# Layer 0's gates by seven quarter products per pair of blocks beside the retention, and its keys, queries and values beside the state space

## The chip, the cores and the metric

The kernel runs on one core of one Trainium2 chip. TensorE multiplies, VectorE (DVE in the profile), ScalarE (ACT) and GpSimd (POOL) do elementwise work, SyncE (SP) issues every DMA of the kernel, in program order, and 16 DMA engines move the bytes. The metric is the device time of one execution in microseconds; 1208.52 is the median of 3 runs of the kernel before (1208.01 to 1209.64).

## The reference

Input x is 1024 frames by 1024 features in float32. Layer 0 normalises x, projects it once (`proj = h @ w_in`) and cuts the result into six parts: the state-space input and its gate (1024 columns each), queries and keys (512 each), values and the retention gate (1024 each).

```
u_s5, g_s5, q, k, v, g_ret = jnp.split(h @ w_in, cuts, axis=-1)
y_s5  = s5_mixer(u_s5, ...) * silu(g_s5)          # state space, gelu, then y * sigmoid(y @ glu_w + glu_b)
y_ret = retention(rope(q), rope(k), v) * silu(g_ret)   # 8 heads, normalised per head
x = x + concat([y_s5, y_ret]) @ w_out
```

Layer 1 is a convolution module with its own projections. A last normalisation gives the output. All of it is float32, and every large product must keep about float32 accuracy.

## The kernel before, in words

Everything lies transposed: 128 features on the partitions, time along the row, so that a block of 128 output features by 512 frames fills one PSUM bank. The 1024 frames make two halves h. Each operand is split into a high part that TensorE's fast float32 format holds exactly and a low part that is the rest; `mm3` (L161) multiplies a 128x128 block of weights with 512 frames in three matmuls: high by high (L166), high weight by low operand (L167), low weight by high operand (L168). `gemm` runs `mm3` over the 8 blocks of the inner dimension, 24 matmuls for one bank. Weights come by `wnext` and `wload` (L105, L114), a list `wseq` in the order of use, two loads ahead: one DMA of 512 KB (tile wf), the high part by ScalarE (wh), the low part by GpSimd or, for the names in `LO_V`, by VectorE (wl). wf, wh and wl have three buffers each.

The work of layer 0 goes in these stages:

- **Front** (`layer0_front`): x is loaded, scaled by norm_g and split into the operands `xs[h][kb]`, 32 tiles of 256 KB that live in the pool opA under the tags A0 (first half) and A1 (second half). The factor of the normalisation (R, along the frames) is multiplied in after the products. Eight blocks of state-space input (u) are made.
- **State space** (`s5_states`, `s5_out`, eight blocks B of 128 features), and beside it the 16 blocks of both gates (`gate_block` in `layer0_front`, two to each B): 48 matmuls of 512 frames to a block, the evacuation by VectorE times R (L349), Silu by ScalarE (L350), a store of 512 KB (L353) to `gs_d` or `gr_d` in DRAM. The blocks' outputs go to `y_d`, and `k_d` holds small tables (Kt) that are stored and read back spread out (Wd).
- **Retention** (`retention`), four pairs of heads. For each pair `ret_proj` makes keys and queries (a `gemm` per half, then the rotation, for which rows are swapped by DMA inside SBUF); values of pairs 0 and 1 come from `ret_values_wide` (matmuls of 512 columns, L930 to L932), those of pairs 2 and 3 from `ret_values` (256 columns, L910 to L912). `y_pass` (L806) reads the state space's output, applies gelu and stores `yn_d`. `ret_heads` (L938) does the attention of two heads (tiles ktp, kv, sp, ro, rt), normalises, multiplies by the gate read from `gr_d` (L998, L1041), and stores `yr_d`.
- **GLU and output projection** (`layer0_back_and_layer1`): `load_split` reads yn_d (operands of the GLU) and later yr_d back, splits them into opA; 16 GLU products follow in the order of blocks nb with both halves h each, with the gate read from `gs_d` (yg, L1094) and multiplied by GpSimd (L1097); then the output projection reads both.

Layer 1 follows. The order of each engine's instructions is decided when the program is built, by a scheduler that goes by priorities and estimated times; each engine then runs its own list strictly in order and waits at semaphores.

## Time and profile before

| | before |
|---|---|
| median of the runs | 1208.52 us |
| span of the profiled execution | 1211.5 us |
| beside the state space (110 to 336 us): TensorE busy | 226.0 of 226 us |
| retention (336 to 590 us): TensorE busy | 252.6 of 254 us |
| GLU and after (590 to 655 us): TensorE busy | 65.0 of 65 us |
| DMA share and rate, 110 to 336 | 0.35, 122 GB/s |
| DMA share and rate, 336 to 590 | 0.59, 187 GB/s |
| DMA share and rate, 655 to 760 | 0.76, 262 GB/s |
| bytes moved by DMA | 227.12 MB |

The span is from the first to the last instruction of one profiled execution; it is its own time, and the median above is of other runs of the same program without a profile. A stage's row counts busy time inside a stretch of the span. The DMA share is the mean busy share of the 16 DMA engines, and the rate is what they moved. Matmuls are pipelined, so that TensorE's busy time overlaps from one to the next; a gap in it is idle time, but a full stretch does not say how fast matmuls follow each other.

### The profile page before, as it was taken

How to read it: one execution, taken by the hardware profiler on the slowest of the kernel's cores; microseconds unless marked ns; L12 is line 12 of the kernel's file. 1: busy time of each engine (PE TensorE's matmuls, PEld its weight loads, DVE VectorE, ACT ScalarE, POOL GpSimd, SP SyncE). 2: the span in 40 equal slices, each digit the busy share in tenths (PEclk: the TensorE clock that was granted, in tenths of full speed). 3: DMA queues.
4: the chain of work that ended last, by engine and by line, in shares of the span. 5: the costliest groups of instructions: out<-in, count | busy, mean ns of one | idle time of the engine just before them, and what ended most of it. 6: DMA issues, size and time to landing. Idle time of an engine off the chain costs nothing.

```text
span 1211.5 us, 17261 instructions
## 1 busy us (share of the span) xinstructions
PE 1199.2 (99%) x6478; PEld 1005.8 (83%) x6478; DVE 756.7 (62%) x1353; ACT 479.7 (40%) x706; POOL 626.5 (52%) x441
## 2 busy tenths in 40 slices
PE   9999999999999999999999999999999999999997
PEld 7888888888888889998888888888888888888877
DVE  7965655555412456457546422699999799899533
ACT  7212233332223232144334322545535675434652
POOL 2059988888236253242341110678453567758642
PEclk9999999999999999999999999999999999999998
DMA  9342433333385175467447886765678654356773
GB/s 334 105 140 72 138 131 136 127 125 141 107 279 181 53 216 141 166 208 257 144 151 235 308 273 218 243 204 201 217 248 276 204 194 153 112 192 234 243 261 131
DMA packets 100516, 227.12 MB, mean 187 GB/s; under 512 B 9296, under 2 KB 38224, under 8 KB 99792
## 3 DMA queue, kind: packets, MB, share of 16 engines
q1 hardware_dynamic: 100432, 226.01, 55.7%
q8 instruction: 51, 0.84, 0.3%
q14 instruction: 33, 0.27, 0.1%
HBM read 160.51 MB, written 61.28 MB: 183 GB/s over the span
## 4 chain that ended last, share of the span: by engine, by line
PE 90%; DMA 5%; DVE 2%; ACT 1%; POOL 1%; issue 1%; SPq 0%; DVEq 0%; POOLq 0%; ACTq 0%
PE mm_g L167 7%; PE mm_g L168 7%; PE mm_g L166 7%; PE mm_wo L166 4%; PE mm_wo L168 4%; PE mm_wo L167 4%; PE mm_b L167 2%; PE mm_b L168 2%; PE mm_a L167 2%; PE mm_a L168 2%; PE mm_b L166 2%; PE mm_a L166 2%; PE mm_u L168 2%; PE mm_u L167 2%; PE mm_u L166 2%; PE mm_oc L167 2%
## 5 line engine op out<-in xcount | busy, mean ns | idle before, releaser
L1225 DVE SCALAR_TENSOR_TENSOR cv<-u,convw,cv 128x512 f32<-128x512 f32 x398 | 273.3, 750 | 12.0 <-ACT cv L1211 9.7
L1205 POOL TENSOR_TENSOR tp<-tp,tp 128x512 f32<-128x512 f32 x64 | 83.2, 1300 | 44.1 <-ACT tp L1204 43.0
L168 PE MATMUL mm_g<-xh,wl_g 128*128 128x512 f32 x256 | 100.8, 394 | 0.0
L167 PE MATMUL mm_g<-xl,wh_g 128*128 128x512 f32 x256 | 100.6, 393 | 0.0
L166 PE MATMUL mm_g<-xh,wh_g 128*128 128x512 f32 x256 | 100.5, 393 | 0.0
L1204 ACT ACTIVATE tp<-u,convw 128x512 f32<-128x512 f32 x64 | 45.7, 720 | 36.5 <-POOL tp L1205 34.9
L349 DVE TENSOR_TENSOR gt<-mm_g,R 128x512 f32<-128x512 f32 x32 | 21.9, 685 | 59.9 <-PE mm_g L168 59.9
L392 POOL TENSOR_TENSOR s1q<-s1q,s1q 128x512 f32<-128x512 f32 x12 | 17.3, 1443 | 78.0 <-ACT s1q L387 78.0
L167 PEld LDWEIGHTS mm_g<-xl,wh_g 128*128 128x128 f32 x256 | 48.1, 188 | 11.3 <-issue 1.6
L168 PEld LDWEIGHTS mm_g<-xh,wl_g 128*128 128x128 f32 x256 | 48.0, 188 | 10.6
L166 PEld LDWEIGHTS mm_g<-xh,wh_g 128*128 128x128 f32 x256 | 48.1, 188 | 9.6
L168 PE MATMUL mm_oc<-zh,wl_woc 128*128 128x512 f32 (+1 forms) x152 | 54.2, 359 | 0.9 <-DMA wl_woc<-lo_woc 0.9
L167 PE MATMUL mm_oc<-zl,wh_woc 128*128 128x512 f32 (+1 forms) x152 | 54.4, 360 | 0.5 <-POOL zl L1050 0.5
L166 PE MATMUL mm_oc<-zh,wh_woc 128*128 128x512 f32 (+1 forms) x152 | 54.1, 361 | 0.0
L1097 POOL TENSOR_TENSOR yg<-yg,yn 128x512 f32<-128x512 f32 x16 | 21.4, 1343 | 59.6 <-DMA yg<-gs_d 25.3
L167 PE MATMUL mm_u<-xl,wh_u 128*128 128x512 f32 x128 | 50.1, 391 | 0.7 <-DVE xl L281 0.6
L166 PE MATMUL mm_g<-h1h,wh_cg 128*128 128x512 f32 x128 | 50.4, 394 | 0.0
L166 PE MATMUL mm_glu<-yh,wh_glu 128*128 128x512 f32 x128 | 50.3, 393 | 0.0
L166 PE MATMUL mm_b<-h1h,wh_cb 128*128 128x512 f32 x128 | 50.2, 392 | 0.0
L166 PE MATMUL mm_wo<-yrh,wh_wor 128*128 128x512 f32 x128 | 50.2, 392 | 0.0
L168 PE MATMUL mm_a<-h1h,wl_ca 128*128 128x512 f32 x128 | 50.2, 392 | 0.0
L166 PE MATMUL mm_wo<-ysh,wh_wos 128*128 128x512 f32 x128 | 50.0, 391 | 0.1
(402 smaller groups left out, 3576.8 us busy)
## 6 DMA issues: line engine op xcount, KB each, us to landing
wf_g<-w_ab SPq DMA_DIRECT2D x16, 512.0 KB, 4.1
wf_wos<-w_out SPq DMA_DIRECT2D x16, 512.0 KB, 4.4
wf_wor<-w_out SPq DMA_DIRECT2D x16, 512.0 KB, 5.6
wf_cb<-w_c SPq DMA_DIRECT2D x16, 512.0 KB, 4.8
wf_ca<-w_c SPq DMA_DIRECT2D x16, 512.0 KB, 4.8
wf_woc<-w_out_c SPq DMA_DIRECT2D x16, 512.0 KB, 5.1
wf_v<-w_v SPq DMA_DIRECT2D x12, 512.0 KB, 5.7
wf_cg<-w_c SPq DMA_DIRECT2D x11, 512.0 KB, 4.3
```

Source lines behind the costliest of these rows:

```text
L166: nc.tensor.matmul(ps, wh[:, kb, :], xh, start=start, stop=False)
L167: nc.tensor.matmul(ps, wh[:, kb, :], xl, start=False, stop=False)
L168: self.last_mm = nc.tensor.matmul(ps, wl[:, kb, :], xh, start=False, stop=stop)
L349: nc.vector.tensor_tensor(gt[:, c], ps[:], self.R[:, c], op=ALU.mult)
L392: nc.gpsimd.tensor_tensor(a, a, sq[:], op=ALU.add)
L1097: gp.tensor_tensor(yg[:], yg[:], yn[:], op=ALU.mult)
L1204: nc.scalar.mul(sk[:], u[:, k:k + HALF], cw[:, nb, k:k + 1])
L1205: gp.tensor_tensor(s0[:], s0[:], sk[:], op=ALU.add)
L1225: v.scalar_tensor_tensor(dst[:], *tap, accs_[i][:], op0=ALU.mult, op1=ALU.add)
```

## The change

The gates are computed by seven products of quarters. Take two neighbouring blocks of gate features (weights split into the halves of the inner dimension) and the two halves of the frames: a two by two by two block product, which eight products of quarters give directly. The change uses seven (Strassen's scheme in Winograd's form), with sums of weights and sums of operands:

- `operand_sums` reads x again beside the state space, scales it by norm_g and R, and forms seven operand sets a0, b0, b1, t1 to t4 (four tiles each, of 128 by 512); each tile is split in a high and a low part (`keep`) and stored in DRAM (`x_d`). `load_set` reads a set back into the tiles of opA.
- `wload_sums` loads the two weights of a pair and forms the sums of their halves by VectorE. It does so twice, since the pairs are gone through in two sweeps: `gates_first` (weights Sa, Sb; sets a0, t2, b0, t1) and `gates_second` (Sc, Sd; sets t3, b1, t4). Partial results of the first sweep go to `part_d` in DRAM and come back in the second, except those of pair 7.
- The sweeps run beside the retention: two pairs ahead of it, the others between its pairs of heads.
- Keys, queries and values (`keys_queries`, `values`) take the gates' place beside the state space, in eight units, one to a block B; all values by matmuls of 512 columns. They are stored in `kq_d`, `v_d` and read back (`ret_rotate`, `ret_values`). The low parts of the values' weights are made by VectorE.
- Gates are stored without Silu. Silu is done by ScalarE when they are read: for the state space at the GLU, for the retention in `load_split` of yr, where GpSimd multiplies.
- The GLU starts with blocks 0 and 1 of the first half; yr's loads are issued behind the sixth and the twelfth load of gates; yn's operands are read into five smaller buffers.

```diff
+    def wload_sums(self, src, name):
...
+            if kind == "a":
+                f = self.w_first = raw(0)
+            elif kind == "b":
+                f, cols = raw(1), (B, A)
+                v.tensor_tensor(f[:, A], f[:, A], f[:, B], op=ALU.add)
+                v.tensor_tensor(f[:, B], f[:, A], self.w_first[:, A], op=ALU.subtract)
+            elif kind == "c":
+                f, g = raw(0), raw(1)
+                v.tensor_tensor(f[:, A], f[:, A], g[:, A], op=ALU.subtract)
+                v.tensor_tensor(f[:, B], f[:, B], g[:, B], op=ALU.subtract)
+                v.tensor_tensor(f[:, B], f[:, B], f[:, A], op=ALU.add)
+                self.w_second = g
+            else:
+                f, cols = self.w_second, (B,)
...
+        for c in cols:
+            h = wh[:].rearrange(fl)[:, c]
+            nc.scalar.copy(h, f[:, c])
+            nc.gpsimd.tensor_tensor(wl[:].rearrange(fl)[:, c], f[:, c], h.bitcast(F32), op=ALU.subtract)
...
-        for nb in range(8, 24):
-            B = (nb - 8) // 2
-            if nb % 2 == 0:
-                self.s5_states(B)
-            gate_block(nb, self.wnext(f"g{nb}"), self.gs_d if nb < 16 else self.gr_d)
-            if nb % 2 == 0 and B:
+        sums = self.operand_sums(xp)
+        for B in range(8):
+            self.s5_states(B)
+            nm, s = UNITS[B]
+            unit = keys_queries(s) if nm == "kq" else values(s)
+            next(unit)
+            for _ in range((B > 0) + (B > 3)):
+                next(sums, None)
+            if B:
                 self.s5_out(B - 1)
-            if nb % 2 and B < 7:
+            for _ in unit:
+                pass
+            for _ in range(2 * (B > 0)):
+                next(sums, None)
+            if B < 7:
                 self.s5_tables(B + 1)
+            if B == 5:
+                self.X = {}
+                self.load_set("a0", "A0")
+                self.load_set("t2", "A0")
         self.s5_out(7)
+        self.load_set("b0", "A1")
+        self.load_set("t1", "A1")
...
+        def keep(f, name, i):
+            hi = xp.tile([P, HALF], F32R, name=f"{name}h_{i}", tag="hi", bufs=2)
+            lo = xp.tile([P, HALF], F32R, name=f"{name}l_{i}", tag="lo", bufs=1)
+            nc.scalar.copy(hi[:], f[:])
+            v.tensor_tensor(lo[:], f[:], hi[:].bitcast(F32), op=ALU.subtract)
+            for q, t in enumerate((hi, lo)):
+                nc.sync.dma_start(self.x_d[name][i, :, q, :], t[:].bitcast(F32))
...
+    def gates_first(self, gp, i):
...
+        wa = self.wnext(f"Sa{i}")
+        x = self.bank(f"mm_g{i}x", aux=False)
+        self.product(x, wa, 0, X["a0"], True)
+        s1 = gp.tile([P, HALF], F32, name=f"gp1_{i}", tag="p1", bufs=1)
+        nc.scalar.copy(s1[:], x[:])
+        wb = self.wnext(f"Sb{i}", ahead=1)
+        z = self.bank(f"mm_g{i}z", aux=False)
+        self.product(z, wb, 1, X["t2"], True)
...
+        part(0)
+        self.wahead(2)
+        self.product(x, wa, 1, X["b0"], False)
+        t = gp.tile([P, HALF], F32, name=f"gc11_{i}", tag="gc", bufs=3)
+        nc.scalar.copy(t[:], x[:])
+        nc.sync.dma_start(self.gate_rows(i, 0)[:, :HALF], t[:])
+        self.product(z, wb, 0, X["t1"], False)
+        part(1)
...
+    def gates_second(self, gp, i):
...
+        self.product(z, wc, 0, X["t3"], True)
+        out(z, 1, 1, 1)
+        x = self.bank(f"mm_g{i}w", aux=False)
+        self.product(x, wc, 1, X["b1"], True)
+        out(x, 1, 0, 1)
+        wd = self.wnext(f"Sd{i}")
+        self.product(z, wd, 1, X["t4"], False)
+        out(z, 0, 1, 0)
...
+        chunks = [first[2:3], first[3:6],
+                  first[6:] + [lambda: self.load_parts(gp, SWEEP2[1]), lambda: sets(("t3", "A0"), ("b1", "A1"), ("t4", "A1"))], second[:4], second[4:]]
         for pair in range(4):
...
+            K, Q, qadds = self.ret_rotate(pair)
+            V = self.ret_values(pair)
+            for f in chunks[pair]:
+                f()
...
-                    v.tensor_tensor(gts[hh][:, c], tp[:], gts[hh][:, c], op=ALU.mult)
+                    nc.scalar.copy(gts[hh][:, c], tp[:])
...
+                        nc.scalar.activation(g, g, AF.Silu)
+                        gp.tensor_tensor(f, f, g, op=ALU.mult)
...
+            nc.scalar.activation(yg[:], yg[:], AF.Silu)
             gp.tensor_tensor(yg[:], yg[:], yn[:], op=ALU.mult)
```

`part(q)` adds the first product to the bank on VectorE and stores the sum (`part_d`); `out` adds the part that came back and stores the quarter of the gate. `product` is four blocks of the inner dimension, 12 matmuls.

More of the change, by code (lines that the diff above doesn't have):

```diff
@@ new lines, in load_set, with gate_rows @@
+    def load_set(self, name, tag):
+        self.X[name] = []
+        for i in range(KB // 2):
+            pair = []
+            for q in range(2):
+                t = self.op_tile(self.opA, tag, f"X{name}{'hl'[q]}_{i}")
+                self.nc.sync.dma_start(t[:].bitcast(F32), self.x_d[name][i, :, q, :])
+                pair.append(t)
+            self.X[name].append(pair)
+    def gate_rows(self, i, n):
+        dst = self.gs_d if i < 4 else self.gr_d
+        k = (2 * i + n) % 8
+        return dst[k * P:(k + 1) * P]
```

295 lines of the change are left out of this document (185 added, 110 removed).

## Prediction

> **What bounds the kernel now.** I read the page first: engine totals, the slices, the chain of work that ended last.
>
> ```profile
> span 1211.5 us, 17261 instructions
> ...
> PE 1199.2 (99%) x6478; PEld 1005.8 (83%) x6478; DVE 756.7 (62%) x1353; ACT 479.7 (40%) x706; POOL 626.5 (52%) x441
> ...
> PE   9999999999999999999999999999999999999997
> ...
> PEclk9999999999999999999999999999999999999998
> DMA  9342433333385175467447886765678654356773
> GB/s 334 105 140 72 138 131 136 127 125 141 107 279 181 53 216 141 166 208 257 144 151 235 308 273 218 243 204 201 217 248 276 204 194 153 112 192 234 243 261 131
> ...
> PE 90%; DMA 5%; DVE 2%; ACT 1%; POOL 1%; issue 1%; SPq 0%; DVEq 0%; POOLq 0%; ACTq 0%
> ```
>
> TensorE is busy 99% of the span and nine tenths or more in 39 of 40 slices, its granted clock is at nine tenths or more in the same slices, and 90% of the chain is TensorE's own work. A microsecond of matmul removed is a microsecond of time, as long as nothing else becomes late. The profiled execution has a span of 1211.5 us, 3.0 over the median of 1208.52; I sum against the span and take 3.0 off.
>
> What else could become late is read from the same columns cut by stage: the state space with the gates beside it (110 to 340), the retention with keys, queries, values (340 to 560), the GLU and the start of the output projection (560 to 700).
>
> ```profile
> core 0: us, PE busy (x) PEld busy (x) DVE busy (x) ACT busy (x) POOL busy (x), PEclk, DMA share, GB/s
> 110.00:340.00 230.00, 230.00 (x1542) 192.51 (x1543) 121.33 (x172) 70.93 (x127) 171.32 (x128) 1.00 0.36 124
> 340.00:560.00 220.00, 220.00 (x1439) 192.21 (x1437) 101.11 (x254) 68.28 (x84) 90.33 (x51) 1.00 0.58 178
> 560.00:700.00 140.00, 138.53 (x667) 115.02 (x664) 76.35 (x133) 51.86 (x76) 40.48 (x24) 0.99 0.65 226
> ```
>
> In the first two stages TensorE never waits, in the third for 1.5 us. VectorE is half busy beside the state space, ScalarE under a third, and the 16 DMA engines are busy 0.36, 0.58 and 0.65 of the time. The change spends exactly these reserves.
>
> How long does a matmul take? The "busy" of one overlaps its neighbour's, so I take start to start: by tile, then by timeline.
>
> ```profile
> L910 PE MATMUL mm_v<-wh_v,xh x128: 277/283/387, 470.1 to 552.3; 128*128 128x256 f32 x128
> ...
> L930 PE MATMUL mm_v<-wh_v,xh x64: 389/389/389, 359.2 to 402.1; 128*128 128x512 f32 x64
> ```
>
> ```profile
> 489.43 0.28 PE L911 MATMUL mm_v<-wl_v,xh 128*128 128x256 f32 x1
> ...
> 490.39 0.28 PE L910 MATMUL mm_v<-wh_v,xh 128*128 128x256 f32 x1
> ```
>
> The 512-wide products of L930 start 64 times between 359.2 and 402.1 us, with the two others of a triple between each pair: 42.9 / (63 x 3) = **0.227 us**. The 256-wide ones make 8 starts in 0.96 us: **0.120 us**, which is more than half of 0.227.
>
> **The change part by part.**
>
> *Matmuls.* Gates: 16 blocks of 48 products (768) become 8 pairs of 7 products of quarters, 12 matmuls each (672): 96 x 0.227 = 21.8 us off. Values: 384 of 256 columns (46.1 us) become 192 of 512 (43.6): 2.5 us off. Keys and queries keep their 384, and everything from the output projection on stays in the same order. The stage beside the state space keeps its length (384 + 384 matmuls in place of 768). If nothing waits: **-24.3 us**, a span of 1187.2. The products that add onto an open bank are matmuls of the same shape; I price them alike.
>
> *Operand sums beside the state space.* Each of 28 quarters is made by VectorE, rounded by ScalarE, its low part subtracted by VectorE, and both parts stored (56 DMAs of 256 KB), after 16 loads of 256 KB. What that costs VectorE:
>
> ```profile
> L349 DVE TENSOR_TENSOR gt<-mm_g,R x32: 676/682/693, 112.5 to 333.7; 128x512 f32<-128x512 f32 x32
> ```
>
> ```profile
> L158 DVE TENSOR_TENSOR wl_g<-wf_g,wh_g 128x1024 fp32r<-128x1024 f32 x13 | 20.5, 1576 | 0.9 <-ACT wh_g L157 0.9
> ...
> L735 DVE TENSOR_TENSOR m<-v,Ts 128x512 f32<-128x512 f32 x8 | 5.5, 692 | 46.3 <-PE v L727 46.3
> ```
>
> Gone are 32 evacuations (21.9 us, L349) and 13 weight subtractions (20.5 us); new are 60 operations of 512 columns (at 0.69 us, 41), 16 evacuations of keys and queries (11) and 16 weight subtractions of the values (16 x 1.58 = 25): 121 - 42 + 77 = 156 of 230 us. As a total this is hidden. As an order it may not be: the low part has **one** buffer. Each of the 28 subtractions waits until the store of the one before has landed, VectorE works in order, and behind the wait stand the evacuations of keys and queries, whose banks TensorE needs for the next values. In the changed program's order nearly all 28 stand between the last u blocks and the third unit of the eight, with 76 us of other VectorE work. Walking that stretch with these durations, each gap between two low parts lasts the longer of the work in it and the landing: 110 us with a landing of 2.2, 120 with 3.0, 137 with 4.0, against some 108 until TensorE wants the bank. How long do stores take?
>
> ```profile
> gs_d<-gt SPq DMA_DIRECT2D x8, 512.0 KB, 4.5
> ...
> gr_d<-gt SPq DMA_DIRECT2D x8, 512.0 KB, 3.4
> ...
> gs_d<-sgg SPq DMA_DIRECT2D x16, 256.0 KB, 3.6
> ...
> outT<-fo SPq DMA_DIRECT2D x8, 256.0 KB, 2.2
> ```
>
> From 2.2 (256 KB, quiet) through 3.6 (256 KB) to 4.5 (512 KB beside S5). The bank waits come to 1.5 us at 2.2, 5 at 2.6, 8 at 3.0, 14 at 3.6 and 30 at 4.5. The new stores are of the size and source of the quiet one, in a stage with 56.0 MB by the program's DMA list instead of 26.1, that is a DMA share of 0.36 x 56.0 / 26.1 = 0.77; I take 2.6, **+5 us**, and keep 0 and 30. SP is in order as well, and this is its worst wait there:
>
> ```profile
> SPq L771 <- ACT Kt L769: 112.5, 8, 14.8
> ```
>
> A low-part store issued behind such a wait adds up to 14.8 us to its own landing; that is why the upper end is as high as 30. The Trainium skill, "DMA: Bandwidth & Descriptors", section "Anatomy of one DMA", says that a DMA pays about 2.0 us of fixed cost, mostly the receipt of the last write, plus its bytes at 436 GB/s. An estimate by that page is 2.6 us for 256 KB, and the term would be 5 us; the rows of 3.6 and 4.5 are above it.
>
> *Gates beside the retention.* This is the large term. Per pair of blocks both weights are loaded twice, two partial results go to DRAM and come back, four raw quarters are stored; keys, queries and values come back from DRAM; five operand sets are loaded. From the changed program's DMA list, from the first load of set b0 up to what the second GLU product needs:
> - weights of the gates 15.7 MB, operand sets 10.5, partials 3.7 + 3.7, raw gates 8.4;
> - keys and queries with their swapped rows 8.4, values 4.2 + 1.0, rope and mask tables 6.0;
> - S5's tail (y out and back, yn, tables) 10.0, normalised retention out 4.2, yn back 4.2, GLU weights and inputs 5.2.
>
> That is **85.2 MB**. In how much time? TensorE's own need from the start of the gates:
>
> ```profile
> L910 PE MATMUL mm_v<-wh_v,xh 128*128 128x256 f32 x128 | 36.4, 284 | 0.0
> ...
> L166 PE MATMUL mm_k<-xh,wh_k 128*128 128x512 f32 x64 | 25.6, 400 | 0.0
> ...
> L930 PE MATMUL mm_v<-wh_v,xh 128*128 128x512 f32 x64 | 24.9, 389 | 0.0
> ...
> L1015 PE MATMUL ro<-v,sc 128*128 128x128 f32 x128 | 18.0, 299 | 0.0
> L166 PE MATMUL mm_glu<-yh,wh_glu 128*128 128x512 f32 x31 | 12.6, 406 | 0.0
> ...
> L983 PE MATMUL sp<-qrot,krot 64*128 64x128 f32 x128 | 10.1, 285 | 0.0
> L1010 PE MATMUL ro<-S,qrot 64*128 64x128 f32 x112 | 9.3, 280 | 1.4 <-DVE sc L989 1.4
> ```
>
> From 336 to 590 us (254 us, no idle but 1.4) stand 384 matmuls of keys and queries and 192 of values at 0.227 (130.8), 384 at 0.120 (46.1) and 93 of the GLU (21.1); the other 56.0 are heads and states. After: 672 x 0.227 = 152.5, plus 56, plus 5.4 for the first GLU product, less some 3 of heads behind it: 211 us. Sets b0 and t1 can load from the last value product on, which stands ahead of the last S5 matmuls: the evacuations of L349 show 31 half blocks in 221.2 us, 7.14 each, of which 24 x 0.227 are gates; the other 1.69 makes 6.8 a block of four halves, and one and a half blocks are left behind, about 11 us. So 85.2 MB in **222 us, 384 GB/s**. What the DMA engines deliver when they are full:
>
> ```profile
> 340.00:360.00 20.00, 20.00 (x90) 16.57 (x89) 2.63 (x4) 5.15 (x4) 6.25 (x4) 1.00 1.01 321
> 672.00:692.00 20.00, 19.94 (x88) 16.04 (x87) 8.86 (x9) 6.66 (x9) 2.93 (x2) 1.00 0.94 327
> 1140.00:1160.00 20.00, 18.56 (x80) 14.36 (x79) 13.74 (x21) 16.12 (x25) 16.89 (x15) 1.00 0.98 358
> 0.00:20.00 20.00, 18.27 (x86) 15.45 (x87) 11.44 (x19) 15.80 (x24) 4.49 (x9) 1.00 0.91 327
> ```
>
> Rate over share: 318, 348, 365, 359 GB/s. At 362 (the two windows whose lines are long, like the new transfers) 85.2 MB take 235 us: **+13**. At 318 to 321 they take 265: +43. At 384 or above: 0. The weights are also split per product pair by ScalarE and GpSimd and summed by VectorE; these have half their time free there, so I price them at nothing while the loads are in time; if DMA is late they are late with it.
>
> One rule speaks against this part. The same page, section "Where 436 GB/s comes from", puts the memory's limit for one core near 358 GB/s and the ports' at 435, and lists 425 GB/s for 16 MB moved by one core alone. By 358 the sum would be 238 us (+16), by 425 it would be 200 and nothing would wait; the window with share 0.98 agrees with the first, and no window here shows the second.
>
> *GLU stage.* Silu moves here, and the retention gate's multiplication:
>
> ```profile
> L350 ACT ACTIVATE gt<-gt 128x512 f32<-128x512 f32 x32 | 20.3, 635 | 32.4 <-DVE gt L349 32.4
> ```
>
> ```profile
> L1097 POOL TENSOR_TENSOR yg<-yg,yn 128x512 f32<-128x512 f32 x16 | 21.4, 1343 | 59.6 <-DMA yg<-gs_d 25.3
> ```
>
> 32 Silu of 0.635 (20 us) on ScalarE and 16 products of 1.34 (21 us) on GpSimd, beside 52 and 40 busy of 140: hidden, but the loads of the gates (4.2 MB) come at a share of 0.65: **+1**, bounds 0 and 6. The 1.4 us stall of the last pair may go; I keep it.
>
> **Sum:** 1211.5 - 24.3 + 5 + 13 + 1 = 1206.2; less 3.0: **1203**.
>
> **The rivals.**
>
> *All hidden.* DMA delivers 384 GB/s or more on average, stores land in 2.2 us. 1187.2 - 3.0 + 1.5, about 1185 (1182 to 1195). For it: loads are issued ahead, and ScalarE, VectorE and GpSimd have room. Against it: no window of 20 us shows 384.
>
> *The transfers become the bound of the retention (slower).* Mixed loads and stores run at what 340 to 360 shows, 321 GB/s at share 1.01, or SP, in order, leaves the queues empty while a store waits for its evacuation. 85.2 / 321 = 265 us, +43; with the other +6, 1233 (1214 to 1240). It decides below 85.2 / (222 + 19) = 354 GB/s: there the time is that of before. For it: the only window that mixes this stage's kinds; over 340 to 560 rate over share is 307. Against it: long lines.
>
> *One buffer for the low part (slower).* Stores land in 3.6 to 4.5 us under the higher load, as two rows do now, and TensorE waits 14 to 30 us at the values' banks beside the state space; with +14 beside the retention 1212 to 1230. From 3.1 us of landing on (+9) there is no gain that can be told.
>
> *The change doesn't do what it says:* if the 96 removed matmuls were not on the path at all. TensorE's 99% excludes that.
>
> **How the numbers follow.** Forecast case, 1203, own range 1196 to 1212: 0.38 (0.26 faster, 0.10 the same, 0.02 slower). All hidden: 0.20. Transfers: 0.24. Low part: 0.18. A measurement of this kernel can tell about 0.2% (2.4 us) from no change. Faster 0.46, same 0.10, slower 0.44. The range leaves a tenth on either side: 1186 to 1236.
>
> **What would show it.** In the changed profile, TensorE's matmuls of 512 columns should start 0.227 us apart and the gates be 672. Right, if idle time of TensorE stands at mm_g products ended by DMA or by weights and sets that wait for DMA, some 13 us, with DMA share over 0.9 beside the retention. "All hidden" shows no such idle time; the transfer rival shows 40 us of it and a share near 1 at 320 GB/s, or less share with SP waiting. The low part shows as VectorE idle until x_d stores land, and TensorE idle at mm_v. I would be wrong altogether if the idle time stood in the GLU or the output projection, or if matmuls ran slower beside the denser transfers, which no row of before can show.

## The result and the profile after

The changed kernel takes 1257.65 us (median of 4 runs, 1253.08 to 1259.88) where the kernel before took 1208.46 beside it: a ratio of 1.0397, with a 95% interval of 1.0374 to 1.0421. That is 49 us slower. The prediction was 1203, its range 1186 to 1236.

The page of the changed kernel, in the order in which that of before was read (totals, slices of TensorE, clock and DMA, the chain):

```profile
span 1256.6 us, 17506 instructions
...
PE 1198.4 (95%) x6190; PEld 982.9 (78%) x6190; DVE 878.8 (70%) x1461; ACT 532.7 (42%) x805; POOL 687.7 (55%) x485
...
PE   9998788999999899999988799999999999999997
...
PEclk9998899999999999999999899999999999999999
DMA  8365656648569999999454798565677745346674
GB/s 326 101 200 177 228 198 225 224 133 288 169 239 340 315 348 289 388 384 329 150 209 143 278 338 270 197 237 192 218 236 262 251 166 192 109 165 229 218 279 156
...
PE 60%; DVE 16%; DMA 16%; issue 3%; ACT 3%; POOL 1%; SPq 1%; DVEq 0%; ACTq 0%; POOLq 0%
```

TensorE's busy total has hardly moved (1199.2 before), although 288 fewer matmuls are recorded, so "busy" tells little here. Its slices tell more: 8 and 7 stand where all were 9, in slices 4 to 7 (94 to 220 us), in 14 and in 21 to 23, and its clock is down to 8 in slices 4, 5 and 23. The chain has lost a third of its TensorE: 60% where it was 90%, and VectorE and DMA hold 16% each.

To see where the time went I cut the span at the first matmul of each stage: the first of w2r (state space), of mm_g0x (gates; in the kernel before, of mm_k, with which its retention starts), of mm_glu, of mm_wo and of mm_b. By tile, of the changed kernel (the last pair of numbers is first and last start in us):

```profile
L942 PE MATMUL w2r<-ident,Mr x32: 270/272/273, 101.5 to 339.0; 128*128 128x128 f32 x32
```

```profile
L201 PE MATMUL mm_g0x<-Xa0h,wh_Sa x4: 389/389/500, 372.1 to 374.3; 128*128 128x512 f32 x4
```

```profile
L224 PE MATMUL mm_glu<-yh,wh_glu x128: 389/389/501, 593.0 to 691.1; 128*128 128x512 f32 x128
```

The same rows of every run give this table; a stage is the difference of two first starts. "Beside S5" is the state space's stage, "to mm_wo" the gates with the retention and the GLU together (before, the GLU's first products stand between the last heads, so that the two do not separate), "mm_wo" the output projection up to layer 1.

| kernel | median us | ratio (95%) | beside S5 | gates/retention | GLU | to mm_wo | mm_wo |
|---|---|---|---|---|---|---|---|
| before | 1208.46 | 1 | 236.0 | | | 318.7 | 106.1 |
| changed | 1257.65 | 1.0397 (1.0374 to 1.0421) | 270.6 | 220.8 | 98.9 | 319.7 | 117.4 |
| pool_light | 1242.57 | 1.0282 (1.0267 to 1.0298) | 260.3 | 217.1 | 97.5 | 314.6 | 118.2 |
| no_lo_store | 1262.04 | 1.0439 (1.0413 to 1.0466) | 273.6 | 221.9 | 98.2 | 320.1 | 117.1 |
| one_set | 1218.03 | 1.0089 (1.0064 to 1.0113) | 236.2 | 215.7 | 98.0 | 313.7 | 116.8 |
| silu_first | 1242.31 | 1.0277 (1.0261 to 1.0292) | 272.2 | 219.9 | 90.1 | 310.0 | 109.8 |
| pool_light_lo3 | 1240.06 | 1.0251 (1.0230 to 1.0271) | 254.3 | 221.6 | 96.7 | 318.3 | 117.0 |
| spread | 1247.72 | 1.0312 (1.0288 to 1.0337) | 259.7 | 217.6 | 99.6 | 317.2 | 115.0 |
| spread_silu | 1237.49 | 1.0244 (1.0209 to 1.0279) | 259.4 | 225.3 | 89.9 | 315.2 | 109.6 |
| no_parts | 1256.06 | 1.0393 (1.0371 to 1.0415) | 271.3 | 214.4 | 99.8 | 314.2 | 116.4 |
| all_three | 1224.15 | 1.0120 (1.0103 to 1.0137) | 236.6 | 220.4 | 100.6 | 321.0 | 115.6 |
| spread_lo2 | 1232.81 | 1.0197 (1.0182 to 1.0212) | 248.2 | 219.1 | 98.1 | 317.2 | 115.4 |
| spread_lo2_silu | 1227.01 | 1.0141 (1.0119 to 1.0162) | 250.0 | 226.6 | 89.8 | 316.4 | 112.0 |
| ld3 | 1251.37 | 1.0342 (1.0319 to 1.0366) | 270.1 | 216.1 | 94.9 | 311.0 | 114.6 |
| light_ret | 1264.90 | 1.0452 (1.0434 to 1.0469) | 274.3 | 221.9 | 99.7 | 321.6 | 117.4 |
| w_no_sum | 1253.71 | 1.0358 (1.0343 to 1.0374) | 271.3 | 214.1 | 98.2 | 312.3 | 118.1 |
| light_w | 1259.97 | 1.0415 (1.0399 to 1.0430) | 272.1 | 220.6 | 100.4 | 321.0 | 114.6 |

The stages are of the one profiled execution, the medians of four runs; a profiled span lies within some 6 us of its kernel's median, so a few us in the stages are not to be matched with the medians. Each kernel is also built anew, with another order of instructions. The seven kernels whose work beside the state space is that of the changed one take 270.1 to 274.3 us there, and the nine whose work beside the retention is the same take 215.7 to 221.9; a difference inside these bounds says nothing. In spans the change costs 45.1 us (1256.6 against 1211.5), and the stages hold it: **34.6** beside the state space, **1.0** up to mm_wo where 24.3 should have been gained, **11.3** in the output projection, and 2 less behind.

The same stages of the changed kernel as windows (columns: window, its length, busy us of each engine with its instructions, granted clock, DMA share, GB/s):

```profile
core 0: us, PE busy (x) PEld busy (x) DVE busy (x) ACT busy (x) POOL busy (x), PEclk, DMA share, GB/s
100.00:371.00 271.00, 248.78 (x1598) 204.24 (x1598) 182.81 (x214) 84.00 (x145) 213.09 (x147) 0.95 0.61 207
129.00:146.00 17.00, 10.37 (x35) 7.69 (x34) 15.84 (x16) 9.71 (x16) 15.43 (x8) 0.70 0.56 184
371.00:592.00 221.00, 210.53 (x1254) 170.37 (x1252) 150.18 (x377) 92.13 (x135) 94.83 (x71) 0.99 1.03 346
592.00:691.00 99.00, 91.97 (x398) 73.90 (x398) 47.24 (x41) 41.13 (x65) 39.45 (x24) 1.00 0.49 171
691.00:808.00 117.00, 109.47 (x468) 88.90 (x467) 52.36 (x55) 44.95 (x62) 32.18 (x25) 0.97 0.77 269
```

Two things are to be seen. The gates' stage (371 to 592) runs with the DMA engines full (share 1.03, 346 GB/s) for 221 us, as the prediction had it. But the largest loss is in the stage ahead of it, where the DMA share is 0.61. TensorE's waits there, by what ended them (total us, times, longest):

```profile
PE v L953 <- ACT W2r L944: 6.2, 1, 6.2
PE mm_v L432 <- DVE ut L395: 4.6, 2, 3.4
PE mm_v L432 <- DVE kraw L416: 3.7, 1, 3.7
PE mm_v L432 <- ACT wh_v L215: 3.6, 1, 3.6
PE mm_v L433 <- DVE wl_v L216: 3.0, 1, 3.0
```

and the largest of VectorE's own for stores:

```profile
DVE t3l L497 <- DMA x_b_d<-b1l: 8.1, 4, 2.8
DVE t2l L497 <- DMA x_b_d<-b0l: 6.0, 3, 2.4
```

So TensorE waits for VectorE (ut, kraw, wl_v), and VectorE waits for the landing of low parts, just as the rival of the one buffer said. But these stores landed in 2.3 to 3.8 us (medians: x_b_d<-b1l 2.3, x_b_d<-b0l 3.0, x_t_d<-t3l 3.8), about where the prediction's rows of 2.2 and 3.6 put them, and at 2.6 it allowed only 5 us.

TensorE also waits for ScalarE, whose own waits between 85 and 240 us are led by these:

```profile
ACT R L924 <- DVE v L968: 20.2, 4, 9.9
ACT b1h L496 <- DVE t1l L497: 14.4, 3, 5.1
ACT b0h L496 <- DVE b1l L497: 11.0, 4, 4.7
ACT t3h L496 <- DVE a0l L497: 10.3, 3, 7.0
```

The high parts have two buffers, and a copy waits until VectorE has made the low part from the one before last. What TensorE needs stands behind these copies: in the timeline b0h starts at 185.2 us after a wait of 4.1, and W2r, TensorE's longest wait of the stage, only behind it at 186.7. R is the R8 of the tables, four scalings to a block.

### The profile page after: what moved, and what is told of

Read it like the earlier page. It is cut to its first block, busy times and chain, and to the rows that moved or that the text cites. A ratio compares the mean times of both kernels' runs of the same rounds, so it can differ in the third digit from the quotient of the medians.

```text
span 1256.6 us, 17506 instructions
## 1 busy us (share of the span) xinstructions
PE 1198.4 (95%) x6190; PEld 982.9 (78%) x6190; DVE 878.8 (70%) x1461; ACT 532.7 (42%) x805; POOL 687.7 (55%) x485
## 4 chain that ended last, share of the span: by engine, by line
PE 60%; DVE 16%; DMA 16%; issue 3%; ACT 3%; POOL 1%; SPq 1%; DVEq 0%; ACTq 0%; POOLq 0%
PE mm_wo L224 4%; PE mm_wo L226 4%; PE mm_wo L225 4%; PE mm_b L226 2%; PE mm_g L226 2%; PE mm_g L224 2%; PE mm_b L225 2%; PE mm_a L226 2%; PE mm_g L225 2%; PE mm_b L224 2%; PE mm_a L224 2%; PE mm_a L225 2%; DMA yg<-gs_d 2%; PE mm_oc L225 2%; PE mm_oc L226 2%
## 5 line engine op out<-in xcount | busy, mean ns | idle before, releaser
L432 PE MATMUL mm_v<-wh_v,xh 128*128 128x512 f32 x128 | 53.0, 421 | 11.8 <-DVE ut L395 4.6
L433 PE MATMUL mm_v<-wl_v,xh 128*128 128x512 f32 x128 | 52.7, 412 | 3.0 <-DVE wl_v L216 3.0
L434 PE MATMUL mm_v<-wh_v,xl 128*128 128x512 f32 x128 | 52.3, 409 | 0.0
L226 PE MATMUL mm_wo<-yrh,wl_wor 128*128 128x512 f32 x128 | 51.2, 400 | 0.8 <-DVE wl_wor L216 0.8
L1288 DVE SCALAR_TENSOR_TENSOR sg<-sg,yg 128x512 f32<-128x512 f32 x16 | 25.6, 1598 | 36.3 <-ACT sg L1287 36.3
L225 PE MATMUL mm_wo<-yrl,wh_wor 128*128 128x512 f32 x128 | 50.6, 395 | 0.0
L225 PE MATMUL mm_wo<-ysl,wh_wos 128*128 128x512 f32 x128 | 50.0, 391 | 0.0
L226 PE MATMUL mm_b<-h1h,wl_cb 128*128 128x512 f32 x128 | 49.9, 390 | 0.0
```

Source lines behind the costliest of these rows:

```text
L225: nc.tensor.matmul(ps, wh[:, kb, :], xl, start=False, stop=False)
L226: self.last_mm = nc.tensor.matmul(ps, wl[:, kb, :], xh, start=False, stop=stop)
L432: nc.tensor.matmul(pss[b][:], xh[:, o], wh[:, k, :], start=kb == 0, stop=False)
L433: nc.tensor.matmul(pss[b][:], xh[:, o], wl[:, k, :], start=False, stop=False)
L434: nc.tensor.matmul(pss[b][:], xl[:, o], wh[:, k, :], start=False, stop=kb == KB - 1)
L1288: v.scalar_tensor_tensor(sg[:], sg[:], 1.0, yg[:], op0=ALU.add, op1=ALU.mult)
```

## The experiments

All kernels start from the changed one.

### What holds the stage beside the state space

**pool_light.** GpSimd makes the state space's tables (26 us to a block in the changed kernel); here they are made once. ScalarE's four scalings to a block (R8) are left out with them, so that GpSimd's work is not all that this run takes away.

```diff
     def s5_tables(self, B):
...
+        if B:
+            self.s5_tab[B] = self.s5_tab0
+            return
```

> Leaves out GpSimd's table work for the state space's blocks 1 to 7 (block 0's tables are used again, so the output is another). Stage beside the state space is 270.6 us in the changed kernel, 236 before. Theory A (VectorE's operations with both inputs in SBUF run slower while GpSimd works): the operand sums and low parts fall from a mean of 1.2 to 1.5 us to 0.7, about 40 us of VectorE come back, the stage falls to 240-247 and the time to about 1230. Theory B (the landing of the single low-part buffer): waits remain, stage 262 or more, time 1248 or more.

Measured: stage 260.3, time 1242.57. Between the two theories: under a third of the loss is gone. VectorE's groups by shape, from 130 to 260 us, of the changed kernel (mean ns of one, then idle before):

```profile
L505 DVE SCALAR_TENSOR_TENSOR xn<-xn,vecs,R 128x512 f32<-128x512 f32 x9 | 11.5, 1279 | 1.3 <-DMA xn<-xT 1.3
...
L523 DVE TENSOR_TENSOR xn<-xn,xn 128x512 f32<-128x512 f32 x3 | 4.4, 1465 | 0.0
...
L497 DVE TENSOR_TENSOR t4l<-xn,t4h 128x512 fp32r<-128x512 f32 x3 | 3.7, 1245 | 2.6 <-DMA x_t_d<-t2l 2.6
...
L963 DVE TENSOR_TENSOR v<-v,Tc 128x512 f32<-128x512 f32 x3 | 2.1, 686 | 0.0
```

and of pool_light:

```profile
L505 DVE SCALAR_TENSOR_TENSOR xn<-xn,vecs,R 128x512 f32<-128x512 f32 x9 | 6.7, 742 | 0.0
L497 DVE TENSOR_TENSOR a0l<-xn,a0h 128x512 fp32r<-128x512 f32 x3 | 4.3, 1427 | 4.9 <-DMA x_t_d<-t1l 4.9
...
L497 DVE TENSOR_TENSOR t4l<-xn,t4h 128x512 fp32r<-128x512 f32 x3 | 2.1, 688 | 2.6 <-DMA x_t_d<-t2l 2.6
L523 DVE TENSOR_TENSOR xn<-xn,xn 128x512 f32<-128x512 f32 x3 | 2.0, 682 | 0.0
```

An operation of VectorE with **both inputs in SBUF** (xn, t4l) takes 1.25 to 1.47 us on average where GpSimd is busy (108.8 of these 130 us in the changed kernel), and 0.68 to 0.74 in pool_light, where it is idle for most of them (busy 17.1). L963, with one input in PSUM, takes 0.69 in the changed kernel, with GpSimd just as busy. The a0l group still takes 1.43 in pool_light, and the timeline says why. Two of VectorE's, then GpSimd's instruction at the first (start, length):

```profile
173.50 2.12 DVE L497 TENSOR_TENSOR a0l<-xn,a0h 128x512 fp32r<-128x512 f32 x1 [1.84 <-DMA x_t_d<-t1l]
...
206.87 0.69 DVE L497 TENSOR_TENSOR a0l<-xn,a0h 128x512 fp32r<-128x512 f32 x1 [3.11 <-DMA x_t_d<-t1l]
```

```profile
172.68 2.39 POOL L216 TENSOR_TENSOR wl_q<-wf_q,wh_q 128x1024 fp32r<-128x1024 f32 x1 [22.07 <-ACT wh_q L215]
```

The same operation takes 2.12 us beside the weight split that GpSimd still makes, and 0.69 at 206.87, where GpSimd does nothing. The durations are as theory A says; the stage gained 10 us where it expected 24 or more.

**no_lo_store.**

```diff
-            for q, t in enumerate((hi, lo)):
-                nc.sync.dma_start(self.x_d[name][i, :, q, :], t[:].bitcast(F32))
+            nc.sync.dma_start(self.x_d[name][i, :, 0, :], hi[:].bitcast(F32))
```

> Leaves out the 28 stores of low parts (the sets are loaded with the high part twice), so that no low part waits for a landing; 7.3 MB less beside the state space. Theory B: the 23 us of VectorE's waits for landings go and the stage beside the state space falls from 270.6 to about 245, time about 1233. Theory A: VectorE stays stretched and 15 to 20 us of the 34 remain, time 1243 to 1248. Theory C (the DMA traffic of the stage itself): in between, as 7 of 56 MB go, 1252.

Measured: stage 273.6, time 1262.04. Nothing came back (270.1 to 274.3 is the spread of like builds), which no theory had expected. VectorE's waits for these landings, some 20 us in the changed kernel, are gone, and TensorE waits as long, for other operations of the same queue:

```profile
PE kt L992 <- DVE Kg L990: 11.5, 2, 7.9
PE mm_v L432 <- DVE ut L395: 7.9, 2, 5.3
```

Kg (a small operation of the state space) and ut (evacuation of the u blocks) are now late: the sums that had waited moved up and stand ahead of them.

**one_set.**

```diff
-            a0, a1 = load(i, 0), load(i, 1)
...
+            keep(load(i, 0), "a0", i)
...
-                self.nc.sync.dma_start(t[:].bitcast(F32), self.x_d[name][i, :, q, :])
+                self.nc.sync.dma_start(t[:].bitcast(F32), self.x_d["a0"][i, :, q, :])
```

> Only the set a0 is made and stored (4 of 28 quarters); all sets are loaded from it, so the loads beside the retention stay. Theories A and B both: the stage beside the state space falls to 240 or less (the sums are the whole loss), time about 1224 to 1228; what is left over before is the 37 us of retention, GLU and output projection less the 24 us of matmuls. If keys, queries and values in the gates' place cost time themselves (theory D), the stage stays above 250 and the time above 1237.

Measured: stage 236.2, time 1218.03 (below the 1224 to 1228 expected). So the sums are the whole loss of this stage; keys, queries and values in the gates' place cost nothing, as predicted.

Three suspects now: slow operations beside GpSimd and waits for landings, neither of which explained the loss alone, and the place in VectorE's order. The next three runs take the first two together, the third alone, and all of them.

**pool_light_lo3.** pool_light, and three buffers for high and low parts, in the room that the tables leave.

```diff
-            hi = xp.tile([P, HALF], F32R, name=f"{name}h_{i}", tag="hi", bufs=2)
+            hi = xp.tile([P, HALF], F32R, name=f"{name}h_{i}", tag="hi", bufs=3)
-            lo = xp.tile([P, HALF], F32R, name=f"{name}l_{i}", tag="lo", bufs=1)
+            lo = xp.tile([P, HALF], F32R, name=f"{name}l_{i}", tag="lo", bufs=3)
```

> Leaves out GpSimd's tables for blocks 1 to 7 as before, and in the room that frees gives the low and high parts three buffers each, so both the slow operations and the waits for landings are gone, with every sum still made. Alone the first took the stage from 270.6 to 260.3 us, and leaving out the low stores left it at 273.6. If the two replace each other in VectorE's queue (theory F: VectorE, in order, is simply too full ahead of the operations TensorE needs, and either cause is enough), the stage falls to 236-246 and the time to 1218-1228. If they add up, 1240 (10 and 0). If something else in the sums holds TensorE (ScalarE's copies, SP's queue), the stage stays at 255 or more and the time above 1237.

Measured: stage 254.3, time 1240.06. Theory F's figures (236 to 246, 1218 to 1228) are missed. The time is the one given for gains that add up, the stage just under the third theory's 255, so these two are not told apart; what is left is 8 us at the first values product, where ut's evacuation stands behind the first sums, and 4 us for wl_v.

**spread.** The sums queued behind each block's state space, and the sets a0 and t2 loaded one block later.

```diff
+        def step():
+            with self.tc.issue_after(self.s5_anchor.ins):
+                next(sums, None)
...
-            for _ in range((B > 0) + (B > 3)):
-                next(sums, None)
...
-            for _ in range(2 * (B > 0)):
-                next(sums, None)
+            for _ in range((2, 2, 2, 2, 3, 3, 2, 0)[B]):
+                step()
```

> The same sums, but their VectorE instructions are queued behind each block's state space (two or three of the sixteen steps to each block 0 to 6, in place of three or four in blocks 1 to 5), and the sets a0 and t2 are loaded one block later; nothing left out. Theory F (the place of the sums in VectorE's queue): the stage beside the state space falls from 270.6 to 240-250 and the time to 1227-1237. If GpSimd's and the stores' slowing are of fixed amount wherever the sums stand, no gain: 1250 or more. Sets that arrive late at the start of the gates would show there as idle TensorE, up to 8 us.

Measured: stage 259.7, time 1247.72. A third of the loss came back, between the two theories; the waits have moved to later blocks. The largest is 7.5 us for W2r, behind ScalarE's copies of high parts again.

**all_three.** pool_light, three buffers, and the spread.

> Takes away all three suspected causes at once: GpSimd's tables of blocks 1 to 7 left out, three buffers for low and high parts, and the sums spread behind each block's state space. Every sum is still made. One by one the stage beside the state space was 260.3 (GpSimd), 273.6 (no low stores), 254.3 (GpSimd and buffers), 259.7 (spread). If these three are the whole cause, 236 to 240 and a time of 1218 to 1226. If the sums hold TensorE in another way as well, 248 or more and 1232 or more.

Measured: stage 236.6, time 1224.15. All of it came back:

```profile
100.00:337.00 237.00, 236.60 (x1601) 197.62 (x1601) 154.06 (x220) 78.06 (x125) 34.53 (x19) 1.00 0.70 242
```

TensorE is busy 236.6 of 237 us although every sum is made. What this run takes away is the whole loss, and it does not add up from single runs: pool_light, no_lo_store and the spread gave 10.3, -3.0 and 10.9 us, all_three 34.0. These suspects lengthen VectorE's queue, for which TensorE waits directly or through ScalarE's, and whichever is left fills the room that another frees. Two things go with them that no run takes alone: R8's scalings, and the third buffer of the high parts. How the 34 us divide among the five is not shown.

**spread_lo2.** The spread, with a second low buffer in the room of one loaded tile; nothing is left out.

```diff
-            lo = xp.tile([P, HALF], F32R, name=f"{name}l_{i}", tag="lo", bufs=1)
+            lo = xp.tile([P, HALF], F32R, name=f"{name}l_{i}", tag="lo", bufs=2)
...
-            t = xp.tile([P, HALF], F32, name=f"xn{kb}_{h}", tag="f", bufs=5)
+            t = xp.tile([P, HALF], F32, name=f"xn{kb}_{h}", tag="f", bufs=4)
```

> The spread sums with two buffers for low parts (one taken from the loaded tiles, four in place of five); nothing left out. With the spread alone the stage was 259.7 us, with VectorE waiting some 20 us for stores to land. If these waits now matter, being no longer covered by a queue that is late anyway: 246 to 252, time 1236 to 1241. If GpSimd's slowing alone holds the rest: 257 or more, 1245 or more.

Measured: stage 248.2, as expected, time 1232.81, 3 us below what was expected. 12 us of the stage's loss are left; all_three, which also leaves out the tables and R8's scalings and has a third buffer for low and for high parts, has none. The landing of low parts, which gave nothing alone, gives 11.5 us once the order is right. TensorE still waits 4.3 us for W2r, behind ScalarE's high parts.

### What holds the GLU and the output projection

TensorE's waits from 590 us on, and ScalarE's in the GLU, of the changed kernel:

```profile
PE mm_glu L224 <- ACT sg L1287: 7.0, 7, 1.8
PE mm_wo L224 <- ACT wh_wor L215: 6.5, 2, 3.3
```

```profile
ACT yg L1282 <- DMA yg<-gs_d: 28.2, 11, 3.6
ACT ysh L1290 <- DVE sg L1288: 19.6, 11, 2.8
```

ScalarE works in order. Its Silu of a gate waits for the gate's load (28.2 us in 11 waits); the Tanh that empties the GLU's bank (sg) stands behind it, and TensorE waits for that bank.

**silu_first.** In the code a condition that always holds stands around the first two additions; it is left out here.

```diff
-        nc.scalar.copy(t[:], x[:])
+        nc.scalar.activation(t[:], x[:], AF.Silu)
...
             v.tensor_tensor(t[:], ps[:], parts[q][:], op=ALU.add)
+            nc.scalar.activation(t[:], t[:], AF.Silu)
...
-            nc.scalar.activation(yg[:], yg[:], AF.Silu)
...
-                        nc.scalar.activation(g, g, AF.Silu)
```

> Silu is done by ScalarE at the evacuation of the gates beside the retention and left out at the GLU and at yr (the output is the same). Theory E (ScalarE, in order, waits for the load of a gate before its Silu, and the GLU's evacuation stands behind): the 9 us lost in the GLU and most of the 11 lost at the start of the output projection come back, some 2 us are lost beside the retention: about 1239. Rival (the loads of gates and yr themselves are late, or VectorE beside GpSimd): no more than 4 us, 1254 or above.

Measured: GLU 90.1 (from 98.9), output projection 109.8 (from 117.4), time 1242.31, 15.3 less. The waits for sg are gone and one for a weight is left:

```profile
PE mm_wo L224 <- ACT wh_wor L215: 1.7, 1, 1.7
```

```profile
592.00:691.00 99.00, 98.96 (x437) 81.62 (x436) 57.07 (x52) 40.32 (x62) 54.96 (x31) 1.00 0.61 206
```

TensorE is busy 98.96 of 99 us in the GLU. Theory E holds; nothing measurable was lost beside the retention (219.9). ScalarE's Silu itself leaves the GLU with this edit too, so the wait and the work are not yet told apart.

**ld3.** Three buffers for the loaded gates. The tag "ld" is also that of tiles of the output projection and of layer 1, which get the third buffer with them.

```diff
-            yg = lp.tile([P, HALF], F32, name=f"yg{nb}_{h}", tag="ld", bufs=2)
+            yg = lp.tile([P, HALF], F32, name=f"yg{nb}_{h}", tag="ld", bufs=3)
```

> The changed kernel with three buffers in place of two for the tiles into which the GLU's gates are loaded; Silu stays at the GLU. Theory E says that ScalarE waits for the gate's load, which waits for the buffer that VectorE's last operation on an earlier gate frees: with a third buffer the load starts one product earlier, ScalarE's wait (28 us over 11 waits) shrinks to a third, and 6 to 9 us of the GLU's loss go: 1248 to 1252. If ScalarE's extra work itself is too much, no gain: 1256 or more.

Measured: GLU 94.9, time 1251.37, 6.3 less. In the GLU 4.0 of 8.8 us came back, short of the 6 to 9 expected. ScalarE's wait for the loads fell only from 28.2 to 22.9 us, TensorE's for sg from 7.0 to 2.8. So the wait for the load is part of the loss, and the rest is not divided between what is left of it and ScalarE's extra work. The time agrees with theory E's, but the retention's stage is 4.7 us shorter in this build, within the spread of builds, so the time is no second proof.

**spread_silu** and **spread_lo2_silu** combine the edits shown.

> The spread sums and the Silu at the gates' evacuation together; nothing left out. Alone the Silu gave 15.3 us. They stand in different stages, so the gains add: the time of the spread sums less 15, 1212 to 1222 if theory F holds. It beats the kernel before only if the stage beside the state space is back to 236.

> The same with Silu at the gates' evacuation. The spread and the Silu together gave 1237.5; with the second buffer 1224 to 1232. Not below 1208 by any theory, as the retention still loses some 16 us of the 24 that the matmuls save.

Measured: 1237.49 and 1227.01. The first is above what was expected (1212 to 1222, on a spread that gave less than hoped). In both the retention's stage is longer than in any other run (225.3 and 226.6), so that part of the Silu's gain is missing there. Whether Silu lengthens that stage is open, since silu_first alone had 219.9. spread_lo2_silu is the fastest version that leaves nothing out, 1.41% slower than the kernel before. No version that beats the kernel before was found.

### What takes the gain back beside the retention

**no_parts.**

```diff
-                nc.sync.dma_start(self.part_d[i, q], t[:])
...
-            self.nc.sync.dma_start(t[:], self.part_d[i, q])
-            self.parts[i].append(t)
+            self.parts[i].append(self.pz)
```

> Leaves out the store and the loading back of the partial gates (28 DMAs, 7.3 MB of some 85 beside the retention; zeros are added in their place). Theory G (the transfers bind the retention, at about 340 GB/s): up to 15 us come back there, time 1242 to 1250. Theory H (TensorE loses there by waits at the start of products and by one late weight, and the DMA engines just keep up): 5 us or less, 1252 or more.

Measured: stage 214.4 (6.4 less, but only 1.3 below the spread of like builds), time 1256.06, within the runs' spread of the changed kernel. The stage speaks weakly for G, the time for H; this run alone decides nothing.

**light_ret.** no_parts, and the tables and values of the first pair used for all.

```diff
-        nc.sync.dma_start(tq[:], A["rope_q"][pair])
+        if pair == 0:
+            ...
+            nc.sync.dma_start(self.tq[:], A["rope_q"][pair])
```

> Leaves out the partial gates' store and load, and the loads of the query tables and of the values for the second to fourth pair (the first pair's are used): 13.6 of some 85 MB beside the retention, 16%. From the gates' start to the first GLU product are 220.8 us in the changed kernel; the matmuls at 0.227 and heads as before would need some 203. Leaving out 7.3 MB gave 214.4. Theory G (transfers bind): 203 to 208, and the time 1240 to 1246. Theory H (single late weights and waits at products' starts): 213 or more, 1251 or more.

Measured: stage 221.9, time 1264.90. The same stretch of 221 us, from the start of the gates:

```profile
L201 PE MATMUL mm_g0x<-Xa0h,wh_Sa x4: 389/389/500, 376.3 to 378.4; 128*128 128x512 f32 x4
```

```profile
375.00:596.00 221.00, 210.05 (x1252) 170.74 (x1250) 151.81 (x373) 88.04 (x132) 99.94 (x71) 0.98 0.85 283
```

The DMA share is down from 1.03 to 0.85, and TensorE's stage is no shorter (221.9 against 220.8), where theory G had 203 to 208. The rate of the transfers does not bind it. Theory H's figure holds.

**w_no_sum** and **light_w.**

```diff
-                v.tensor_tensor(f[:, A], f[:, A], f[:, B], op=ALU.add)
-                v.tensor_tensor(f[:, B], f[:, A], self.w_first[:, A], op=ALU.subtract)
...
-                v.tensor_tensor(f[:, A], f[:, A], g[:, A], op=ALU.subtract)
-                v.tensor_tensor(f[:, B], f[:, B], g[:, B], op=ALU.subtract)
-                v.tensor_tensor(f[:, B], f[:, B], f[:, A], op=ALU.add)
```

> Leaves out VectorE's sums of the weights (40 operations; raw weights are split and multiplied), all transfers stay. Theory I (the weights' way through VectorE, ScalarE and GpSimd, each in order behind other work, makes them late): the stage from the gates' start to the first GLU product falls from 220.8 to 212 or less, time 1245 to 1250. Theory G: 219 or more, 1254 or more.

> Both left out. If transfers and the weights' way are two causes, their gains add; if one stands behind the other, the stage is where the better of the two was. At best 203 us and 1238 to 1242.

Measured: w_no_sum 214.1 and 1253.71; light_w 220.6 and 1259.97. The first moves 6.7 us in theory I's direction, not as far as it said and only 1.6 us below the spread of like builds; the second, which leaves out the same sums and 13.6 MB more, moves nothing. So theory I is neither shown nor refuted. The stage went between 214 and 227 us over all runs without a rule that these runs show. What can be said from the changed kernel's trace: its 672 gate matmuls take 167.5 us from start to start where 672 x 0.227 are 152.5; 9 us of the difference are gaps of more than 0.15 us. TensorE's two longest waits of the stage are these:

```profile
PE mm_g4z L201 <- ACT wh_Sb L190: 4.3, 1, 4.3
PE kv L1147 <- DMA v<-v_d: 1.3, 1, 1.3
```

The other 6 us are 0.1 to 0.2 us at the start of many of the 12-matmul products. The heads take 55.9 us of start to start, 51.4 before. The wait for wh_Sb is a queue's again: VectorE had summed the weight at 433.7 us, and ScalarE split its second half only at 437.7, behind the load of a function table (1.28 us), an activation and two copies. Six other kernels show the same wait with 3.7 to 3.8 us; in the rest others stand in its place. Counted as above, the gaps of over 0.15 us come to 4 us in w_no_sum and 14 in light_ret, where no wait for a DMA stands among TensorE's.

So the loss beside the retention is shown not to be the rate of the transfers; that it is the sum of many waits in queues is read from traces, and which edit would take them away **stays open**.

## Why the prediction was wrong, step by step

- **What bounds the kernel; the matmuls.** Right as far as it went. The cadence of undisturbed products is 0.227 us in the changed trace too, and the stage beside the state space is as long as before when the sums are left out (236.2 against 236.0).
- **Operand sums, +5, measured +34.6.** This is the step that failed first and most. It priced "60 operations of 512 columns (at 0.69 us, 41)" from L735, whose input v lies in PSUM; the new operations read two inputs from SBUF beside a GpSimd that is busy 213 of the stage's 271 us, and take 1.25 to 1.5 us there. The Trainium skill says as much: "GPSIMD Engine Reference", section "Specifications", has the SBUF interfaces of GpSimd shared with VectorE, with contention for VectorE's instructions with two SBUF inputs. The traces agree (1.25 against 0.69 for t4l), and that section gives no size. VectorE was busy 182.8 us of the stage where the step had 156 of a shorter one. The row of the right kind was quoted beside it, L158, with both inputs in SBUF; but at 1576 ns for 1024 columns it would have given 0.79 us for 512, not 1.25 to 1.5. And the total was not what bound: 182.8 of 271 us would still fit. What failed is the step from a total that fits to one wait as the only price of the queue.
- **The landing of the low part.** Right in duration (2.3 to 3.8 us), wrong as a price: the walk took the landing as the only thing that could stretch the queue. The place of the sums counts as much. They stand ahead of the evacuations and of Kg in VectorE's order, as could be read from the changed program, and the walk looked at one bank wait only. It left out the high parts, whose two buffers hold up ScalarE, and with it W2r (6.2 us). The estimate of 2.6 us that it put beside its rows from the Trainium skill, "DMA: Bandwidth & Descriptors", section "Anatomy of one DMA", rests on a fit that this section gives for DMAs issued by GpSimd; here SyncE issues them, and the medians are 2.3 to 3.8 us.
- **Transfers beside the retention, +13.** About the right size for the wrong reason. Up to mm_wo 25.3 us of the 24.3 + 1.0 are lost; 8.8 of them the GLU's, so 16 to 17 here. The DMA engines were full as forecast (a share over 0.9, measured 1.03), and the rate was 346 GB/s where 362 was taken. But TensorE itself waited only 1.3 us for a DMA, and with 13.6 MB less the stage was no shorter; that the term is near 16 is luck. The limit of 358 GB/s that the prediction took from the Trainium skill ("DMA: Bandwidth & Descriptors", "Where 436 GB/s comes from") lies above the mean, 346, but two slices in a row of the changed page (503 to 565 us) show 388 and 384 GB/s, so it is no limit here, and the prediction's "no window of 20 us shows 384" held for the kernel before alone. The longer stage that followed from the limit was not borne out.
- **GLU, +1, measured 8.8 (98.9 less 90.1).** The step counted ScalarE's busy time and called it hidden. It did not name what is queued behind the waiting instruction: ScalarE's Silu waits for a load, and the evacuation of a bank stands behind it. silu_first shows that the Silu's place is the cause, and ld3 that the wait for the load is part of it.
- **The output projection, no term, measured 11.3.** 7.6 of it came back with silu_first, so it is the same queue: the split of wh_wor stands behind the Silu of yrg. The other 3.7 is not explained. The prediction had said that idle time in the GLU or the output projection would show it wrong altogether, and both have it.
- **The rivals.** The low-part rival had the right engine and stage, and its upper end, 30, was short of the loss because the slow operations were in no case. "All hidden" and "transfers" did not happen. The range failed since no case had all stages late, and none the output projection: terms of 35, 17, 9 and 11 us came together.

## What to carry to other kernels

Price a VectorE operation from a row whose operands lie in the same memories, with the same neighbour busy: here two inputs in SBUF beside a busy GpSimd cost about twice what one in PSUM did. An engine's reserve as a share of its stage says nothing about an engine that works in order; walk the queue, and ask of every instruction that can wait what stands behind it and who waits for that. Where several causes lengthen one queue, taking away one can show little or nothing, so take them away together before one is acquitted. Before a gain of a few us is credited to an edit, look how far builds differ whose work in that stage is the same: here by 4 us in one stage and 6 in another.

## What the runs showed of the hardware that was not expected

VectorE's operations with two SBUF inputs had no fixed price in the changed kernel (a0l: 675 ns the shortest, 2456 the longest of four), and went with what GpSimd did at the time, while those of the same size with one input in PSUM kept theirs (kraw and qraw 0.67 to 0.69; ut, which writes in another order, 1.06 to 1.19, before the change 1.11 to 1.16).

A wait of TensorE costs more than itself. After two stops of over 3 us the timeline of TensorE in the changed kernel goes on like this (start, length):

```profile
134.24 1.61 PE L432 MATMUL mm_v<-wh_v,xh 128*128 128x512 f32 x4 [3.58 <-ACT wh_v L215]
138.91 0.80 PE L433 MATMUL mm_v<-wl_v,xh 128*128 128x512 f32 x1 [3.05 <-DVE wl_v L216]
139.50 0.63 PE L434 MATMUL mm_v<-wh_v,xl 128*128 128x512 f32 x1
139.93 0.63 PE L432 MATMUL mm_v<-wh_v,xh 128*128 128x512 f32 x1
140.35 0.63 PE L433 MATMUL mm_v<-wl_v,xh 128*128 128x512 f32 x1
140.78 0.63 PE L434 MATMUL mm_v<-wh_v,xl 128*128 128x512 f32 x1
```

From 139.50 on the starts are 0.42 to 0.43 us apart, not 0.227, and the granted clock is 0.50 from 134.8 to 145.0 us. Beside the state space 24 matmuls ran so, 4.8 us on top of the waits. The Trainium skill, "TensorE: Matmul & The Clock Gate", section "What's actually happening", describes half clock after an idle window of about 3.4 us and until the array has been busy as long; the half rate and the stop of 3.58 us agree. The half clock stands before the second stop begins, and the starts are 0.23 us apart again from 145.05, 6.1 us after that stop ended.
